# The turned rows in two steps with early masked values, and another weight and hold for the last two pairs' chains

## The chip, the core and the metric

The kernel runs on one core of a Trainium2 chip. A run's time is the device time in microseconds of one execution. The profile shows one execution of the program as recorded by the hardware profiler: TensorE (PE for matmuls, PEld for its weight loads), VectorE (DVE), ScalarE (ACT), GpSimd (POOL) and SyncE (SP, here the issuer of DMAs).

## The reference

The kernel computes a two-layer streaming encoder on 512 frames of 1024 features in float32. Layer A mixes time with a gated recurrence (12 heads of 64) beside a four-head attention into 256 memory tokens; layer B uses chunked attention beside another memory attention. After each mixer comes an output projection and a gated feed-forward block with a three-tap convolution. The change touches only layer A's recurrence:

```python
def wkv7_scan(r, w, k, v, a, b):
    ...
    def step(state, inp):
        r_t, w_t, k_t, v_t, a_t, b_t = inp
        sa = jnp.einsum('bhvk,bhk->bhv', state, a_t)
        state = (state * w_t[:, :, None, :] + sa[..., None] * b_t[:, :, None, :]
                 + v_t[..., None] * k_t[:, :, None, :])
        return state, jnp.einsum('bhvk,bhk->bhv', state, r_t)
    s0 = jnp.zeros((bsz, nh, hd, hd), jnp.float32)
    _, ys = lax.scan(step, s0, xs)
```

Here `a` is the negative normalised key and `b` that key times a learned gate. The result is normalised per head, a bonus term is added, and the whole is multiplied by a gate.

## The kernel before

The 512 frames form eight chunks of 64, and the 12 heads form six pairs (0 to 5), two heads to the 128 partitions. Inside a chunk the recurrence becomes small matmuls; only a short chain runs from chunk to chunk. Three generators do a pair's work.

`prepare(i)` projects the pair's r, k, v and gates: lora-gate matmuls (L740 to L743), then dense matmuls in three products (L204, L205 with the high half of the weights, L208 with the low half). It scans the decay on VectorE (L778) and exponentiates it on ScalarE (L779, L781, with a copy L780). It then makes the key scores (L807); ScalarE copies them (L812), SyncE writes them to DRAM (L815) and reads them back turned as `Lr` (L821); VectorE solves small triangular systems in a chain of short instructions (L830 to L843); the result goes through DRAM again (L849) and returns as `Tc` (L853).

`front(i)` makes the masked chunk scores `ML` (matmuls L898, eviction on VectorE L901), then the turned rows: `rows_av()` turns a and v for the even chunks in two banks (`ev`, L923/L925, copies L928) and the odd chunks in one (`od`, L932/L935, copies L938); `rows_kb()` turns the keys (L913, copies L916). After that it waits for the next pair's scores and extends the inverse to 32 rows (L968, L985, with the copies L974, L977 and L990 of `Y` and `Tt` on ScalarE).

`back(i)` extends the inverse to 64 rows and applies it: transposes on VectorE (L1017); b1X (L1022, copies L1027); the masked values, a product of `ML` and `VT` (L1031, copies L1033); b2Tt (L1038, copies L1042); b3W (L1046, copies L1048 and L1050); b4MQ (L1056, evicted on VectorE by L1058 and L1060); b5G (L1067, L1068, and the copy L1069); b6y (L1077). The chunk-to-chunk chain follows (L1082 on TensorE, L1083 on VectorE, L1087 for the output), then the head norm (L1091 to L1098, sums L690, and via L696 the transposes L699), the bonus and the gate (L1105 to L1116).

All short matmuls write to banks of one PSUM pool with four banks, handed out in turn in program order. Two more pools hold dense results and the chain.

The order is set by `weave()`. It holds a list of generators with a weight each. A generator that is not on hold and has used the smallest share of its weight goes next; each `yield cost` or `yield cost, hold` adds cost to a common clock, and hold keeps the generator back for that much of it. In this way the program order of all instructions is fixed when the kernel is built, and each engine executes its own in a fixed order. In the stages 0 to 4 of the first mixer, `weave` joins the front of pair s, the preparation of pair s + 1, and the back of pair s - 1:

```python
gens = [(front(st_, Ts[st_], Ts[st_ + 1]), 1.069 * FRONT_COST), (prepare(st_ + 1, Ts[st_ + 1]), .971 * PREP_COST)]
if st_ > 0:
    gens.insert(0, (back(st_ - 1, Ts[st_ - 1], dst_mix), 1.003 * BACK_COST))
weave(gens, tc)
```

In this text a stage runs from one L740 to the next; stage 2 begins at 116.0 us, stage 3 at 169.0. The last weave (L1215 to L1223) joins the back of pair 4, the chain of front and back of pair 5, the memory queries and attention, and the first part of the output projection. The dense matmuls of the others are what TensorE has between the short steps.

Of the kernel before, what the change touches and what calls it, by code (L numbers as in the profile page):

```python
# [18 lines left out]
P = 128  # L19
# [63 lines left out]
def weave(gens, tc=None):  # L83

    live = [[g[0], float(g[1]), 0.0, 0.0, g[2] if len(g) > 2 else 0, None] for g in gens]
    now = 0.0
    while live:
        free = [e for e in live if e[5] is None or e[5]()]  # L90
        ready = [e for e in free if e[3] <= now]
        if not ready:
            now = min(e[3] for e in free)
            continue
        e = min(ready, key=lambda x: x[2] / x[1])
        e[5] = None
        try:
            with tc.high_priority(e[4]) if e[4] else ExitStack():
                y = next(e[0])
        except StopIteration:  # L100
            live.remove(e)
            continue
        if callable(y):
            e[5] = y
            continue
        cost, wait = y if isinstance(y, tuple) else (y, 0)
        now += cost
        e[2] += cost
        e[3] = now + wait
# [3 lines left out]
def trunk_kernel(ctx, tc, A, out):  # L113
    nc = tc.nc
    PE, V, SC, GP = nc.tensor, nc.vector, nc.scalar, nc.gpsimd
# [29 lines left out]
    def ps_s(shape=(P, S)):  # L145
        return banks["S"].tile(list(shape), F32, name="pss", tag="pss")
# [355 lines left out]
    HS = (top, bot)  # L502
# [47 lines left out]
    for m in range(KD):  # L550
        nc.sync.dma_start(xs[m // 2][:, m % 2], A["xT"][:, m])
        if m in (0, 2):
            u = slice(m * 256, m * 256 + 512)
# [150 lines left out]
    MC = 16 * 80  # L704
# [7 lines left out]
    def four():  # L712

        for c2 in range(4):
            for par in range(2):
                for h in range(2):
                    c = c2 * 2 + par
                    yield c, c2, par, h, slot(c, h)

    def par_of(t, par):  # L720

        return t.rearrange("p (a e) t -> p a e t", e=2)[:, :, par]
# [164 lines left out]
    def front(i, T, nxt=None):  # L887
        v, KB, AR, Tt, Lc, Tc = c3(T["v"][:]), T["KB"], T["AR"], T["Tt"], T["Lc"], T["Tc"]

        ML = kt_("ML", (P, 2, NCH, 192), bufs=2)  # L890

        for c4 in range(2):
            ps = [ps_s((P, 4, 128)) for _ in range(2)]
            for c in range(4):
                cc = c4 * 4 + c
                for h in range(2):
                    u = slot(cc, h)
                    PE.matmul(ps[h][:, c], KB[HS[h], cc, 1 - u:3 - u].rearrange("p s t -> p (s t)"),  # L898
                              AR[HS[h], cc].rearrange("p s t -> p (s t)"), start=True, stop=True)
            for h in range(2):  # L900
                V.tensor_tensor(ML[:, h, c4 * 4:c4 * 4 + 4, 0:128], ps[h][:],  # L901
                                C("m1").unsqueeze(1).to_broadcast([P, 4, 128]), op=ALU.mult)
            yield 1000
        Rq = kt_("Rq", (P, 8, 64), bufs=2)
        SC.copy(Rq[:], AR[:, :, 1, :])
        VT = kt_("VT", (P, 3, NCH, 64), bufs=2)

        def rows_kb():
            ps = [ups(), ups()]
            for c in range(8):  # L910
                for h in range(2):
                    u = slot(c, h)
                    PE.transpose(ps[h][:, c], KB[HS[h], c, 1 - u:3 - u].rearrange("p s t -> p (s t)"),  # L913
                                 cst[HS[h], I64:I64 + 64])
            for h in range(2):
                SC.copy(ML[:, h, :, 128:192], ps[h][:])  # L916


        def rows_av():
            ev = [ps_s((P, 4, 128)) for _ in range(2)]  # L920
            for c2 in range(4):
                for h in range(2):
                    PE.matmul(ev[h][HS[h], c2, 0:64], AR[HS[h], c2 * 2, 0], cst[HS[h], I64:I64 + 64], start=True, stop=True)  # L923
                for h in range(2):
                    PE.matmul(ev[h][HS[1 - h], c2, 0:64], v[HS[h], c2 * 2], C("blkc", h * 64, 64)[HS[h]],  # L925
                              start=True, stop=True)
            for h in range(2):
                SC.copy(par_of(VT[:, h], 0), ev[h][:, :, 0:64])  # L928
            od = ps_s((P, 2, 4, 64))
            for c2 in range(4):  # L930
                for h in range(2):
                    PE.matmul(od[HS[h], h, c2], AR[HS[h], c2 * 2 + 1, 0], cst[HS[h], I64:I64 + 64],  # L932
                              start=True, stop=True)
                for h in range(2):
                    PE.matmul(od[HS[h], 1 - h, c2], v[HS[h], c2 * 2 + 1], C("blkc", h * 64, 64)[HS[h]],  # L935
                              start=True, stop=True)
            for n in range(2):
                SC.copy(par_of(VT[:, n], 1), od[:, n])  # L938

        rows_av()  # L940
        yield 1000
        rows_kb()
        yield 800


        if nxt is not None:
            yield lambda: "scores" in nxt
        else:
            yield 0, 9000

        def tied():
            order = ExitStack()
            for ins in (dense_at[0],) if nxt is None else (nxt["keys"], *nxt["scores"]):
                order.enter_context(tc.issue_after(ins.ins))
            return order

        Tn = kt_("Tn", (P, NCH, 32))
        with tied():
            tn = V.transpose(Tn[:].rearrange("p c s -> p (c s)"), Tc[:].rearrange("p c s -> p (c s)"))
        if nxt is None:  # L960
            tc.keep_in_program_order(tn)
        ps = ps_s((P, 8, 16))
        for c2 in range(0, 8, 2):
            with tied():
                for c in (c2, c2 + 1):
                    for u in range(4):
                        rw = slice(u * 32, u * 32 + 32)
                        PE.matmul(ps[rw, c], Lc[rw, c], Tc[rw, c, 16:32], start=True, stop=True,  # L968
                                  tile_position=(u * 32, u * 32))
            if c2 < 6:  # L970
                yield 200
        Y = kt_("Y", (P, NCH, 16))
        with tied():
            SC.copy(Y[:], ps[:])  # L974
            for u in range(4):
                rw = slice(u * 32, u * 32 + 32)
                tt = SC.copy(Tt[rw, :, u % 2 * 32:u % 2 * 32 + 32], Tc[rw])  # L977
                if nxt is None and u == 0:
                    tc.keep_in_program_order(tt)
        yield 200, 600  # L980
        ps = ps_s((P, 8, 16))
        for c in range(8):
            for u in range(4):
                rw = slice(u * 32, u * 32 + 16)
                PE.matmul(ps[rw, c], Tn[rw, c, 0:16], Y[rw, c], start=True, stop=True, tile_position=(u * 32, u * 32))  # L985
            if c in (1, 3, 5):
                yield 200
        for u in range(4):
            rw = slice(u * 32, u * 32 + 16)
            SC.copy(Tt[rw, :, u % 2 * 32 + 16:u % 2 * 32 + 32], ps[rw])  # L990
        yield 200
        T.update(Rq=Rq, ML=ML, VT=VT)

    FRONT_COST = 2 * 1000 + 1000 + 3 * 800

    def own_tiles():

# [12 lines left out]
    def back(i, T, dst, tiles=own_tiles, go=None):  # L1010
# [3 lines left out]
        for par in range(2):  # L1014
            for h in range(2):
                u = h ^ par
# [7 lines left out]
        for par in range(2):  # L1024
            for h in range(2):
                hi_ = slice(h * 64 + 32, h * 64 + 64)
                SC.copy(par_of(X5[hi_], par), ps[par][hi_, :, 0:32])  # L1027
        yield 650
        ps = [ps_s((P, 4, 128)) for _ in range(2)]
        for c, c2, par, h, u in four():  # L1030
            PE.matmul(ps[par][HS[h], c2, 0:64], ML[HS[1 - u], h, c, 0:64], VT[HS[1 - u], u, c], start=True, stop=True)  # L1031
        for par in range(2):
            SC.copy(par_of(VT[:, 2], par), ps[par][:, :, 0:64])  # L1033
        yield MC / 2
        ps = ups()
        for c, h, ap, vp in U:
            lo, hi_ = slice(h * 64, h * 64 + 32), slice(h * 64 + 32, h * 64 + 64)
# [12 lines left out]
                SC.copy(par_of(VT[HS[u], u], par), ps[par][HS[u], :, 1])  # L1050
        yield 1100
        G, St = VT[:, 2], W
        yield 0, 900
        ps = [ps_s((P, 4, 128)) for _ in range(2)]
        for c, c2, par, h, u in four():
            PE.matmul(ps[par][HS[h], c2], W[HS[u], c], ML[HS[u], h, c, 64:192], start=True, stop=True)  # L1056
# [8 lines left out]
        for c, h, ap, vp in U:  # L1065
            u = slot(c, h)
# [41 lines left out]
        dst(i, yc, pg)  # L1108
        yield 1080

    BACK_COST = 2 * 650 + 1.5 * MC + 2 * 1100 + 1700 + 6 * 150 + 7 * 150 + 700 + 1080

    mixd = dp.tile([4, P, S], F32, name="mixd", tag="mixd")

# [26 lines left out]
    def chain(*gs_):  # L1141
        for g in gs_:
            yield from g
# [59 lines left out]
    over = set()  # L1203

    def later(ns):
        yield 0, ns

    def told(g, n):
        yield from g
        over.add(n)  # L1210

    def ahead():
# [2 lines left out]

    AHEAD = [0, 1, 2, 3, 4, 6, 7]
    a_, b_ = NPAIR - 2, NPAIR - 1
    weave([(told(back(a_, Ts[a_], dst_mix), "back"), 1.5 * BACK_COST),
           (chain(front(b_, Ts[b_]), later(6000), back(b_, Ts[b_], dst_mix, other_tiles, lambda: "back" in over)),
            1.5 * (FRONT_COST + BACK_COST)),  # L1220
           (told(chain(q_mem(lambda f: A["wA"][18 + f], hact, qmA), flush_mix(), mA), "mem"),
            16 * 648 + mem_cost(860)),
           (ahead(), 14 * 648)], tc)  # L1223
# [346 lines left out]
```

## Time and profile before

| | before |
|---|---|
| median of three runs | 1351.67 us (1349.16, 1351.67, 1352.93) |
| the profiled execution's own time | 1350.19 us |
| its span in the trace | 1348.4 us |
| mean granted TensorE clock | 0.989 |
| DMA | 135.41 MB, mean 100 GB/s |

In the views that follow, a row of a timeline gives the start in us, the duration in us, the engine, the line, the operation, the tile written and those read, and in brackets the idle time of that engine before the row and what ended it. Rows of consecutive equal instructions are joined (x8). A row by window gives its length, then the busy time of PE, PEld, DVE, ACT and POOL, the granted clock (1.00 is full), the DMA share and GB/s.

### The profile page before, as it was taken

How to read it: one execution, taken by the hardware profiler on the slowest of the kernel's cores; microseconds unless marked ns; L12 is line 12 of the kernel's file. 1: busy time of each engine (PE TensorE's matmuls, PEld its weight loads, DVE VectorE, ACT ScalarE, POOL GpSimd, SP SyncE). 2: the span in 40 equal slices, each digit the busy share in tenths (PEclk: the TensorE clock that was granted, in tenths of full speed). 3: DMA queues.
4: the chain of work that ended last, by engine and by line, in shares of the span. 5: the costliest groups of instructions: out<-in, count | busy, mean ns of one | idle time of the engine just before them, and what ended most of it. 6: DMA issues, size and time to landing. Idle time of an engine off the chain costs nothing. (4 is left out here: it accounts for less than half of the span.)

```text
span 1348.4 us, 24498 instructions
## 1 busy us (share of the span) xinstructions
PE 1311.2 (97%) x9838; PEld 1099.4 (82%) x9838; DVE 927.0 (69%) x1834; ACT 688.8 (51%) x1196; POOL 20.5 (2%) x45
## 2 busy tenths in 40 slices
PE   9998999999999999999999999999999999999996
PEld 6786777777788899998888878787788999988886
DVE  7966566765568998889333666658589888893224
ACT  6666556756445444456222566657444444562221
POOL 0000000000000000000000000000000000000000
PEclk9999999999999999999999999999999999999998
DMA  5365333433042432322323422232224222223322
GB/s 195 109 185 106 76 86 85 112 85 88 1 172 83 136 123 66 124 65 88 102 86 91 157 87 80 86 109 86 94 78 156 93 96 95 94 75 100 102 86 77
DMA packets 65729, 135.41 MB, mean 100 GB/s; under 512 B 19792, under 2 KB 25296, under 8 KB 65616
## 3 DMA queue, kind: packets, MB, share of 16 engines
q1 hardware_dynamic: 63168, 124.94, 29.4%
q0 software_dynamic: 2448, 8.91, 3.7%
q8 instruction: 77, 1.26, 0.4%
q14 instruction: 36, 0.29, 0.1%
HBM read 127.53 MB, written 6.29 MB: 99 GB/s over the span
## 5 line engine op out<-in xcount | busy, mean ns | idle before, releaser
L176 DVE TENSOR_TENSOR wlo<-wraw,whi 128x1024 fp32r<-128x1024 f32 (+1 forms) x139 | 165.6, 1192 | 143.9 <-PE psd L208 131.6
L170 ACT CAST whi<-wraw 128x1024 fp32r<-128x1024 f32 (+1 forms) x156 | 159.8, 1026 | 162.0 <-DMA wraw<-in_ffn_out_dram 42.0
L204 PE MATMUL psd<-r1h,whi 128*128 128x512 f32 (+1 forms) x383 | 152.9, 401 | 0.1
L205 PE MATMUL psd<-r1l,whi 128*128 128x512 f32 x320 | 126.7, 397 | 0.0
L170 ACT CAST whi<-raw 128x1024 fp32r<-128x1024 f32 x88 | 82.9, 943 | 80.7 <-PE psf L420 45.5
L176 DVE TENSOR_TENSOR wlo<-raw,whi 128x1024 fp32r<-128x1024 f32 x88 | 95.8, 1088 | 15.5 <-ACT whi L170 15.2
L208 PE MATMUL psd<-r1h,wlo 128*128 128x512 f32 (+1 forms) x383 | 103.3, 396 | 0.0
L204 PEld LDWEIGHTS psd<-r1h,whi 128*128 128x128 f32 x383 | 72.3, 189 | 16.2 <-issue 1.7
L208 PEld LDWEIGHTS psd<-r1h,wlo 128*128 128x128 f32 x383 | 68.6, 188 | 13.4 <-issue 0.2
L420 PE MATMUL psf<-r2l,whi 128*128 128x256 f32 x308 | 77.2, 283 | 0.0
L420 PE MATMUL psf<-r2h,whi 128*128 128x256 f32 x308 | 77.2, 283 | 0.0
L204 PE MATMUL psd<-r2h,whi 128*128 128x512 f32 (+1 forms) x184 | 71.1, 390 | 0.1
L238 ACT ACTIVATE tmp<-xT 128x512 f32<-128x512 f32 x27 | 17.1, 632 | 104.8 <-DVE xT L497 89.0
L205 PEld LDWEIGHTS psd<-r1l,whi 128*128 128x128 f32 x320 | 60.5, 189 | 11.6 <-issue 0.5
L205 PE MATMUL psd<-r2l,whi 128*128 128x512 f32 (+1 forms) x184 | 69.9, 383 | 0.0
L420 PEld LDWEIGHTS psf<-r2l,whi 128*128 128x128 f32 x308 | 59.1, 192 | 0.2
L420 PEld LDWEIGHTS psf<-r2h,whi 128*128 128x128 f32 x308 | 59.1, 192 | 0.2
L422 PE MATMUL psf<-r2h,wlo 128*128 128x256 f32 x308 | 49.5, 283 | 0.0
L208 PE MATMUL psd<-r2h,wlo 128*128 128x512 f32 (+1 forms) x184 | 47.1, 386 | 0.0
L204 PE MATMUL psd<-hl,whi 128*128 128x512 f32 (+1 forms) x119 | 44.4, 377 | 0.0
L205 PE MATMUL psd<-sl,whi 128*128 128x512 f32 (+1 forms) x119 | 44.4, 377 | 0.0
L205 PE MATMUL psd<-hl,whi 128*128 128x512 f32 (+1 forms) x119 | 44.3, 376 | 0.0
(473 smaller groups left out, 3323.4 us busy)
## 6 DMA issues: line engine op xcount, KB each, us to landing
wraw<-in_ffn_in_dram SPq DMA_DIRECT2D x44, 512.0 KB, 3.7
raw<-in_ffn_in_dram SPq DMA_DIRECT2D x88, 256.0 KB, 3.8
wraw<-in_ffn_out_dram SPq DMA_DIRECT2D x32, 448.0 KB, 3.3
wraw<-in_wA_dram SPq DMA_DIRECT2D x20, 512.0 KB, 4.3
wraw<-in_w_out_dram SPq DMA_DIRECT2D x16, 512.0 KB, 3.9
wraw<-in_ffn_out_dram SPq DMA_DIRECT2D x16, 512.0 KB, 3.5
wlo<-in_wA_dram POOLq DMA_DIRECT2D x15, 512.0 KB, 7.7
wraw<-in_wB_dram SPq DMA_DIRECT2D x8, 512.0 KB, 3.5
```

The lines of the kernel that those rows point to most:

```text
L170: SC.copy(hi[:, :n], raw)
L176: V.tensor_tensor(lo[:, :n], raw, hi[:, :n], op=ALU.subtract)
L204: PE.matmul(ps, wh[:, j * P:(j + 1) * P], ah, start=start and n == 0, stop=False)
L205: dense_at[0] = PE.matmul(ps, wh[:, j * P:(j + 1) * P], al, start=False, stop=False)
L208: dense_at[0] = PE.matmul(ps, wl[:, j * P:(j + 1) * P], act(k)[0], start=False, stop=stop and n == len(ks) - 1)
L238: SC.activation(sq[:], src, AF.Square)
L420: PE.matmul(ps, wh[:, o + k * P:o + k * P + P], x[k][n], start=k == n == 0, stop=False)
L422: PE.matmul(ps, wl[:, o + k * P:o + k * P + P], x[k][0], start=False, stop=k == 3)
```

## The change

Four things change; no instruction is added, removed or given another shape.

- The turned rows become two steps: `rows_av()` now ends after the even chunks, and the odd chunks are a function of their own, `rows_odd()`, with a yield between, and `rows_kb()` comes last. There are holds of 1000 after the first step and after the keys.
- The masked values move from `back()` to `front()`, behind the turned keys. In `back()` the yield after b1X becomes `400, 800`.
- In `back()` the hold before b4MQ goes from 900 to 2000.
- In the last weave both chains get 4 in place of 1.5 as the factor of their weight, and the hold between the last pair's front and back goes from 6000 to 2000. The cost totals follow the moved yields.

```diff
         rows_av()
-        yield 1000
+        yield 550, 1000
+        rows_odd()
+        yield 1080
         rows_kb()
-        yield 800
+        yield 800, 1000
+        ps = [ps_s((P, 4, 128)) for _ in range(2)]
+        for c, c2, par, h, u in four():
+            PE.matmul(ps[par][HS[h], c2, 0:64], ML[HS[1 - u], h, c, 0:64], VT[HS[1 - u], u, c], start=True, stop=True)
+        for par in range(2):
+            SC.copy(par_of(VT[:, 2], par), ps[par][:, :, 0:64])
+        yield MC / 2
...
-    FRONT_COST = 2 * 1000 + 1000 + 3 * 800
+    FRONT_COST = 2 * 1000 + 1630 + 3 * 800 + MC / 2
...
                 SC.copy(par_of(X5[hi_], par), ps[par][hi_, :, 0:32])
-        yield 650
-        ps = [ps_s((P, 4, 128)) for _ in range(2)]
-        for c, c2, par, h, u in four():
-            PE.matmul(ps[par][HS[h], c2, 0:64], ML[HS[1 - u], h, c, 0:64], VT[HS[1 - u], u, c], start=True, stop=True)
-        for par in range(2):
-            SC.copy(par_of(VT[:, 2], par), ps[par][:, :, 0:64])
-        yield MC / 2
+        yield 400, 800
...
-        yield 0, 900
+        yield 0, 2000
...
-    BACK_COST = 2 * 650 + 1.5 * MC + 2 * 1100 + 1700 + 6 * 150 + 7 * 150 + 700 + 1080
+    BACK_COST = 400 + 650 + MC + 2 * 1100 + 1700 + 6 * 150 + 7 * 150 + 700 + 1080
...
-    weave([(told(back(a_, Ts[a_], dst_mix), "back"), 1.5 * BACK_COST),
-           (chain(front(b_, Ts[b_]), later(6000), back(b_, Ts[b_], dst_mix, other_tiles, lambda: "back" in over)),
-            1.5 * (FRONT_COST + BACK_COST)),
+    weave([(told(back(a_, Ts[a_], dst_mix), "back"), 4 * BACK_COST),
+           (chain(front(b_, Ts[b_]), later(2000), back(b_, Ts[b_], dst_mix, other_tiles, lambda: "back" in over)),
+            4 * (FRONT_COST + BACK_COST)),
```

In the changed file the lines behind the turned rows move by up to ten: `od` is L934/L937, the masked values L950 with the copies L952, b1X L1032, b2Tt L1042, b3W L1050, b4MQ L1060, b5G L1071, b6y L1081, the chain L1086. In the prediction a line's number is that of the kernel before, unless it says otherwise.

More of the change, by code (lines that the diff above doesn't have):

```diff
@@ L928, in rows_av, with rows_odd @@
                 SC.copy(par_of(VT[:, h], 0), ev[h][:, :, 0:64])
+        def rows_odd():
             od = ps_s((P, 2, 4, 64))
```

## The prediction

> **What bounds the kernel now.** I read the page first, then the waits of TensorE, then the busy time by window, cut at the first lora-gate matmul (L740) of each stage, and last the timelines of the few places where TensorE idles. A difference under 0.3% (4 us) cannot be told from no change here.
>
> ```profile
> PE 1311.2 (97%) x9838; PEld 1099.4 (82%) x9838; DVE 927.0 (69%) x1834; ACT 688.8 (51%) x1196; POOL 20.5 (2%) x45
> ```
> ```profile
> PE pss L932 <- DVE MQ L1060: 5.0, 4, 3.9
> PE pss L1056 <- ACT W L1048: 2.8, 6, 0.7
> ```
> ```profile
> 116.00:169.00 53.00, 46.57 (x668) 35.65 (x666) 31.63 (x106) 30.04 (x61) 3.45 (x4) 0.94 0.41 88
> 169.00:213.60 44.60, 42.11 (x655) 31.91 (x654) 29.77 (x97) 28.38 (x60) 2.59 (x3) 1.00 0.41 93
> ```
>
> The two waits listed are TensorE's longest around the change (total us, times, longest). TensorE is busy 97% of the span, so the kernel is as long as its matmuls, TensorE's idle time, and what a low granted clock adds. The change keeps every instruction and its shape; only the order moves. So I count just idle time and clock in the stages of the first mixer. In the windows (columns: length, busy PE, PEld, DVE, ACT, POOL, granted clock, DMA share, GB/s) stage 2 (116 to 169) takes 53.0 us and stage 3, with the same kinds of work, 44.6; the granted clock is 0.94 against 1.00. That 8.4 us is the one large loss that an order could give back.
>
> **Stage 2: what the loss is, and what the change does to it.**
>
> ```profile
> 113.10 0.35 SPq L181 DMA_DIRECT2D wraw<-in_wA_dram  x1
> 113.62 1.73 SPq L821 DMA_DIRECT2D Lr<-d  x4
> ```
> ```profile
> DMA to landing us min/median/max: 1.6/1.8/6.9
> ```
> ```profile
> 121.83 0.36 DVE L830 TENSOR_TENSOR Xu<-Lr,cst 128x120 f32<-128x120 f32 x1 [2.17 <-DMA Lr<-d]
> ```
> ```profile
> 121.34 1.48 PE L1046 MATMUL pss<-VT,Tt 64*64 64x128 f32 x32 [1.35 <-ACT Tt L1042]
> 132.05 0.48 PE L932 MATMUL pss<-cst,AR 64*64 64x64 f32 x4 [3.86 <-DVE MQ L1060]
> ```
> ```profile
> 58.00:60.00 2.00, 0.00 (x0) 0.00 (x0) 2.00 (x5) 1.29 (x2) 0.00 (x0) 1.00 0.34 43
> 62.00:64.00 2.00, 1.74 (x9) 1.74 (x10) 2.00 (x5) 1.90 (x6) 0.00 (x0) 0.64 0.08 8
> 64.00:66.00 2.00, 2.00 (x11) 2.00 (x11) 2.00 (x3) 0.17 (x1) 0.00 (x0) 0.51 0.17 17
> 132.00:134.00 2.00, 1.95 (x33) 1.86 (x33) 0.56 (x2) 1.28 (x3) 0.00 (x0) 0.50 0.66 94
> ```
>
> SyncE issues a weight load of 512 KB and then the four small reads of Lr (L821). One of these took 6.9 us to land where the median is 1.8. VectorE therefore starts its chain on Lr (L830 to L843) only at 121.83; the evictions of MQ stand behind that chain on VectorE, and L932, which takes MQ's banks, waits 3.86 us for them. After that gap the clock stood at 0.50. With the 1.35 us of L1046 the stage loses 5.2 us of idle, and the rest, 3.2 of the 8.4, is the half clock.
>
> In the changed kernel as built, SyncE lists the four Lr reads ahead of that weight load, and ScalarE lists the copies of the lora scores that feed them ahead of an L762 that stood before them. With the median landing instead of 6.9, Lr arrives about 5 us earlier, the chain on VectorE ends before MQ is wanted, and the Tt copy (L1042, now L1046) no longer stands behind the exponentials L779 and L781. I take 6.5 us of the 8.4: all of it less the 1.9 that the new wait at a stage's head, priced below, costs in this stage too. The bounds are 8.4, and nothing if the late landing comes from something other than that load. Moving the load behind the reads costs SyncE's queue 1.73 us; weights are buffered ahead, so I take nothing, at most that 1.7.
>
> **Heads of stages 3, 4 and 5: a wait is added.** The listed order after the norm transposes (L699) was: L1031, b2Tt (L1038), scores (L898), b3W (L1046), three dense, b4MQ (L1056), ev (L923/925), od (L932/935). It becomes: b2Tt, three L208 and a dense, b3W, scores, ev, b4MQ, one dense, b5G (L1067), two dense, od.
>
> ```profile
> 163.77 1.98 PE L208 MATMUL psd<-r1h,wlo 128*128 128x512 f32 x8
> 166.28 0.63 PE L699 MATMUL pss<-cst,tmp 128*128 128x128 f32 x4 [0.53 <-DVE tmp L696]
> 170.11 0.68 PE L1031 MATMUL pss<-VT,ML 64*64 64x64 f32 x16
> 171.77 0.69 PE L1038 MATMUL pss<-Tt,X 32*32 32x32 f32 x32
> 173.49 1.10 PE L1046 MATMUL pss<-VT,Tt 64*64 64x128 f32 x32
> 174.52 0.50 PE L205 MATMUL psd<-r1l,whi 128*128 128x512 f32 x1
> 176.21 0.65 PE L1056 MATMUL pss<-ML,W 64*64 64x128 f32 x6 [0.72 <-ACT W L1048]
> 177.25 0.77 PE L1056 MATMUL pss<-ML,W 64*64 64x128 f32 x19 [0.39 <-ACT W L1048]
> 179.11 0.33 PE L932 MATMUL pss<-cst,AR 64*64 64x64 f32 x4 [0.31 <-DVE MQ L1060]
> ```
> ```profile
> 164.90 0.69 DVE L882 TENSOR_TENSOR bon<-pss,v 128x512 f32<-128x512 f32 x1
> 172.63 1.23 DVE L778 TENSOR_TENSOR_SCAN tmp<-acc,tmp 128x512 f32<-128x512 f32 x1
> ```
> ```profile
> 175.79 0.37 ACT L1048 COPY W<-pss 128x256 f32<-128x256 f32 x1
> 177.09 0.74 ACT L1050 COPY VT<-pss 64x256 f32<-64x256 f32 x2
> ```
>
> There are four small banks, taken in turn, so ev takes the two banks of b3W, which the copies L1048/L1050 free. Those copies stand on ScalarE behind three instructions that wait for the decay scan (L778); they ended at 177.83, 11.55 us after L699 began. Without the L1031 block TensorE reaches ev sooner: before, L699 to the end of b3W took 8.24 us (166.28 to 174.52); less the L1031 block and the dense matmul inside it (170.11 to 171.77, 1.66) and plus five L208 (0.25 each from the row of eight), one dense and the bonus matmuls (2.1 together, the last 0.85 an estimate) it is about 8.65. The scan is no earlier, and with L882 moved behind L696 about 0.6 later (0.69 by its row), so the copies end at about 12.2. ev alternates between its two banks and must wait for the last one: 3.3 us idle, and about 0.5 more at b4MQ, whose banks are freed by an eviction (L901) that is listed near the end of VectorE's chain. Before, the same stretch idled 0.72 + 0.39 + 0.31 = 1.4. The net is 2.4 per stage; if the scan is not later it is 1.4. I take 1.9, so 5.7 for three stages (bounds 0 and 7.2: at zero, the copies are as early as TensorE).
>
> The gap may also drop the clock: an idle of about 2.2 us around 58 to 60 was followed by 0.64 and 0.51 at 62 to 66, and the 3.86 above by 0.50. Stage 2's half clock cost 3.2, so I price one fall at 2 us and give it an even chance: 3 us over three stages (0 to 6). [...]
>
> **The tail (pairs 4 and 5, 295 to 366).** Weights of 4 and a hold of 2000 put the chains in front of the dense work.
>
> ```profile
> 309.51 0.39 PE L205 MATMUL psd<-r1l,whi 128*128 128x512 f32 x1
> 309.74 0.39 PE L204 MATMUL psd<-r1h,whi 128*128 128x512 f32 x1
> 295.59 0.66 PE L699 MATMUL pss<-cst,tmp 128*128 128x128 f32 x4 [0.35 <-DVE tmp L696]
> 300.18 1.16 PE L898 MATMUL pss<-AR,KB 64*128 64x128 f32 x16 [0.50 <-DVE ML L901]
> 323.48 0.33 PE L1082 MATMUL psl<-W,MQ 64*64 64x64 f32 x4 [0.55 <-DVE W L1083]
> 334.15 1.98 PE L1046 MATMUL pss<-VT,Tt 64*64 64x128 f32 x32
> ```
> ```profile
> 295.45 0.74 DVE L763 SCALAR_TENSOR_TENSOR v<-tmp,vec,v 128x511 f32<-128x511 f32 x1
> 296.11 0.34 DVE L830 TENSOR_TENSOR Xu<-Lr,cst 128x120 f32<-128x120 f32 x1
> 297.77 0.79 DVE L836 SCALAR_TENSOR_TENSOR Xsb<-Lr,Xsb 128x14 f32<-128x14 f32 x5
> 328.40 1.28 DVE L1017 STREAM_TRANSPOSE AR<-Tt 32x128 f32<-32x128 f32 x4
> ```
> ```profile
> 312.11 1.39 ACT L977 COPY Tt<-Tc 32x256 f32<-32x256 f32 x3 [0.72 <-DMA Tc<-d2b]
> ```
> ```profile
> 332.00:342.00 10.00, 10.00 (x125) 7.62 (x119) 3.83 (x11) 4.99 (x17) 0.00 (x0) 0.51 0.17 54
> ```
>
> Before, dense matmuls (0.23 us each, 309.51 to 309.74) lie between nearly all steps, and waits on this stretch add up to about 2.4 us. After, L696 stands on VectorE behind L760, four transposes, L763, L830 to L836 and two more, by the rows above 0.74 + 0.34 + 0.79 + 1.28 and, estimated from their like, 1.4 for the rest: 4.5 us. Sixteen dense and three L208 (16 x 0.23 + 3 x 0.25 = 4.4) stand on TensorE for that and for the rsqrt steps ahead of it, which at 0.2 us each of some eight (estimated) take 1.5: 1.6 idle. Then come, with no dense work between, the second scores and ev waiting for L901 (2.1 by the 0.5 of 300.18 for each of four steps), b4MQ and b5G (0.7), and the first state step, whose W copy stands on ScalarE behind L977's wait for a DMA (1.6): 6.0. The last pair's b-steps, listed without memory scores between them, add about 3. So 9.0 - 2.4 = +6.6 (bounds: 2, if VectorE catches up, and 11). The clock can go either way: at 332 to 342 it stood at 0.51 after state steps and memory scores with only the short waits shown, and L1046 took 1.98 instead of 1.10, so about 4.5 us was lost there; the dip may go, or a second one may come at 301 to 316 (+3). I net these to -0.6, so the tail is +6.
>
> **Sum.** -6.5 + 5.7 + 3 + 6 = +8.2 on the profiled 1350.19, which is 1358.4 us; that execution lies 1.5 under the median of 1351.67 and inside the three runs. Predicted: 1358.5.
>
> **Rivals.** *The dips decide, faster.* Stage 2 gives 6.5, the 332 dip goes (-4.5) since memory work now interleaves with the state steps, the copies are hardly late (+1.5 in three stages), and the tail idles half of my sum (+3.3): -6.2, so 1344. For it: both dips are in the trace, and every idle I add rests on listed order alone. Against: ev needs both banks. It decides if W's copies come before about 9.2 us after L699. Chance 0.24. *It cancels.* Stage 2 gives 6.5, the heads cost 5.7 with no clock fall because no gap reaches 3.86 us, the one gap of this length in stage 2, and the tail's 6.6 loses the dip of 4.5: +1.3, so 1351.5. Chance 0.20. [...] *The clock falls everywhere:* three heads and the tail, +3 and +3 more: 1365. Chance 0.14. *The change does not do what it says in stage 2:* Lr still lands late, and since L830 now stands ahead of the scan, the scan waits too: the 6.5 is lost and the heads cost the same, 1365. Chance 0.05.
>
> **How the numbers follow.** My forecast has 0.37; with the last two, slower has 0.56, same 0.20, faster 0.24. The range reaches from the faster case to a little past the clock case: 1343.5 to 1367.5. The forecast's own range is 1354 to 1363.
>
> **What would show it.** Right: stage 2 near 46 us with no half clock, L821 landing near 1.8 us at most; ev (L923) waiting on W or VT copies by 2 to 3.5 us in stages 3, 4 and 5; L699 waiting 1 to 2 us near 296; L977's successor late. Wrong: stages 3 to 5 at or below 44.6 us, or no dip after 330.

## Result: slower by 0.3%, half of what was summed

| | before | after |
|---|---|---|
| median | 1349.17 us (20 runs, 1347.66 to 1352.93) | 1353.31 us (20 runs, 1347.68 to 1359.08) |
| ratio | | 1.0032, 95% interval 1.0021 to 1.0044 |
| profiled execution | 1350.19 us, span 1348.4 | 1352.74 us, span 1351.0 |

The 20 runs of the changed kernel spread over 11 us, those before over 5, and by and large the longer runs have the lower granted clock: 0.994 in the one of 1347.68 us, 0.983 in the one of 1359.08. The clock goes with the spread: the correlation of span with (1 - clock) x span over the 20 runs is 0.93.

The busy times and TensorE's longest waits around the change, after:

```profile
PE 1313.0 (97%) x9838; PEld 1101.3 (82%) x9838; DVE 925.6 (69%) x1834; ACT 688.9 (51%) x1196; POOL 20.2 (1%) x45
```
```profile
PE pss L923 <- ACT VT L1054: 5.0, 6, 1.1
PE psl L1086 <- ACT W L1073: 3.8, 1, 3.8
PE pss L699 <- DVE tmp L696: 1.9, 5, 0.7
PE pss L995 <- issue: 1.5, 2, 1.0
```

The waits on MQ (5.0) and on W (2.8) that were shown before are gone, and ev (L923) waits in their place, six times, 5.0 us in all. One single wait of 3.8 us is new. Stages 2, 3 and 4, cut again at L740:

```profile
117.75:163.71 45.96, 45.01 (x668) 33.82 (x667) 32.81 (x108) 29.21 (x60) 2.59 (x3) 1.00 0.47 100
163.71:208.46 44.75, 42.25 (x655) 32.01 (x654) 29.96 (x97) 28.15 (x59) 2.59 (x3) 1.00 0.40 92
208.46:255.41 46.95, 43.52 (x655) 33.18 (x654) 29.98 (x97) 28.37 (x59) 2.59 (x3) 0.96 0.39 84
```

The differences between the two profiles, from one L740 to the next: start +1.5 (ahead of every line that the change touches; a piece of half clock that costs 1.7 us stands there at 9), stages 0 and 1 +0.2 together, stage 2 -7.0 (52.95 to 45.96), stage 3 +0.15, stage 4 +2.35, and from stage 5's L740 to the end of the span +5.4 (1090.21 to 1095.59). Together +2.6, which is the difference of the spans. The medians differ by 4.1, because the profiled run before lies 1.0 above its median and the one after 0.6 below.

The stretch behind stage 5's L740 can be parted at the next norm transposes (L699, at 295.59 before and 296.62 after), where the tail of the prediction begins:

```profile
258.19:295.59 37.40, 35.47 (x586) 27.03 (x585) 26.01 (x82) 24.33 (x52) 1.72 (x2) 1.00 0.34 81
255.41:296.62 41.21, 37.77 (x598) 28.91 (x597) 26.60 (x91) 25.89 (x53) 2.59 (x3) 1.00 0.40 89
```

The first row is before, the second after. More matmuls stand in this part after the change, so its length tells nothing. TensorE's idle time does: 3.4 us in place of 1.9. So 1.5 of the 5.4 belongs to stage 5 with its head, and 3.9 to what lies behind it, the tail.

The reads of Lr for stage 2 on SyncE's queue, and the time that all such reads took to land, after:

```profile
113.62 1.70 SPq L821 DMA_DIRECT2D Lr<-d  x4
115.48 0.35 SPq L181 DMA_DIRECT2D wraw<-in_wA_dram  x1
```
```profile
DMA to landing us min/median/max: 1.6/2.9/4.2
```

The reads stand ahead of the weight load now, as forecast. The head of stage 3, after, on TensorE and on ScalarE:

```profile
159.24 0.66 PE L699 MATMUL pss<-cst,tmp 128*128 128x128 f32 x4 [0.32 <-DVE tmp L696]
160.67 0.50 PE L208 MATMUL psd<-r1h,wlo 128*128 128x512 f32 x1
161.10 1.15 PE L898 MATMUL pss<-AR,KB 64*128 64x128 f32 x8
...
166.57 1.47 PE L1050 MATMUL pss<-VT,Tt 64*64 64x128 f32 x32
167.97 1.16 PE L898 MATMUL pss<-AR,KB 64*128 64x128 f32 x16
170.10 0.27 PE L923 MATMUL pss<-cst,AR 64*64 64x64 f32 x1 [0.97 <-ACT VT L1054]
171.13 0.27 PE L923 MATMUL pss<-cst,AR 64*64 64x64 f32 x1 [0.59 <-ACT VT L1054]
```
```profile
170.34 0.74 ACT L1054 COPY VT<-pss 64x256 f32<-64x256 f32 x2
```

ev waits for the last copies of b3W, as forecast, but for 1.56 us and not 3.3. In stages 4 and 5 it waits 1.65 and 1.76:

```profile
214.85 0.27 PE L923 MATMUL pss<-cst,AR 64*64 64x64 f32 x1 [1.06 <-ACT VT L1054]
215.89 0.27 PE L923 MATMUL pss<-cst,AR 64*64 64x64 f32 x1 [0.59 <-ACT VT L1054]
261.64 0.33 PE L923 MATMUL pss<-cst,AR 64*64 64x64 f32 x2 [1.05 <-ACT VT L1054]
262.67 0.27 PE L923 MATMUL pss<-cst,AR 64*64 64x64 f32 x1 [0.71 <-ACT VT L1054]
```

And in the tail, the new large wait, on ScalarE and on TensorE, and then the granted clock:

```profile
313.02 1.40 ACT L987 COPY Tt<-Tc 32x256 f32<-32x256 f32 x3 [3.72 <-DMA Tc<-d2b]
314.44 0.24 ACT L1073 COPY W<-VT 128x64 f32<-128x64 f32 x1
```
```profile
314.74 0.33 PE L1086 MATMUL psl<-W,MQ 64*64 64x64 f32 x4 [3.78 <-ACT W L1073]
```
```profile
216.00:218.00 2.00, 2.00 (x56) 1.70 (x56) 1.80 (x7) 1.83 (x4) 0.00 (x0) 0.80 1.00 194
218.00:220.00 2.00, 2.00 (x25) 1.46 (x25) 1.24 (x4) 0.75 (x2) 0.00 (x0) 0.50 0.69 113
316.00:318.00 2.00, 2.00 (x12) 1.26 (x8) 0.87 (x2) 0.58 (x1) 0.00 (x0) 0.55 0.01 4
334.00:336.00 2.00, 2.00 (x30) 1.67 (x29) 1.96 (x7) 0.69 (x3) 0.00 (x0) 0.50 0.59 217
```

ScalarE takes L1073 behind three copies that wait 3.72 us for a DMA; TensorE has no other work ahead of it in its order. Half clock follows that gap at 316, comes once in stage 4 (217 to 221) and again at 333 to 341.

### The profile page after: what moved, and what is told of

It reads as the page before. It is cut to its first block, busy times and chain, and to the rows that moved or that the text cites. A ratio compares the mean times of both kernels' runs of the same rounds, so it can differ in the third digit from the quotient of the medians.

```text
span 1351.0 us, 24483 instructions
## 1 busy us (share of the span) xinstructions
PE 1313.0 (97%) x9838; PEld 1101.3 (82%) x9838; DVE 925.6 (69%) x1834; ACT 688.9 (51%) x1196; POOL 20.2 (1%) x45
## 5 line engine op out<-in xcount | busy, mean ns | idle before, releaser
L208 PE MATMUL psd<-r1h,wlo 128*128 128x512 f32 (+1 forms) x383 | 106.5, 400 | 0.0
L208 PEld LDWEIGHTS psd<-r1h,wlo 128*128 128x128 f32 x383 | 68.8, 189 | 13.9 <-issue 0.2
L422 PE MATMUL psf<-r2h,wlo 128*128 128x256 f32 x308 | 49.5, 283 | 0.0
L208 PE MATMUL psd<-r2h,wlo 128*128 128x512 f32 (+1 forms) x184 | 47.1, 386 | 0.0
L204 PE MATMUL psd<-hl,whi 128*128 128x512 f32 (+1 forms) x119 | 44.4, 377 | 0.0
L420 PE MATMUL psf<-r1h,whi 128*128 128x256 f32 x176 | 44.2, 284 | 0.2 <-ACT tmp L442 0.2
```

The source lines that it names most:

```text
L204: PE.matmul(ps, wh[:, j * P:(j + 1) * P], ah, start=start and n == 0, stop=False)
L208: dense_at[0] = PE.matmul(ps, wl[:, j * P:(j + 1) * P], act(k)[0], start=False, stop=stop and n == len(ks) - 1)
L420: PE.matmul(ps, wh[:, o + k * P:o + k * P + P], x[k][n], start=k == n == 0, stop=False)
L422: PE.matmul(ps, wl[:, o + k * P:o + k * P + P], x[k][0], start=False, stop=k == 3)
```

## The measure that the experiments use

Summed over windows of 1 us, 1 - clock is taken here as the time that a stretch of half clock takes away; before, the 32 matmuls of b3W took 1.10 us at a clock of 1.00 (at 173.49) and 1.98 at 0.50 (at 334.15). Ahead of the kernel's last microseconds it comes in pieces of 1.7 us, or two, three or six times that, in the profiles of both kernels and of e9 to e14: 3.4 us at half clock lose 1.7. Before, it was 1.7 at 62, 3.4 at 130 to 138, 5.1 at 332 to 343; after, 1.7 at 9, 63, 217 and 316, 3.4 at 333.

So each run can be parted into (1 - clock) x span and the rest. A run's clock is on record to 0.001, which is 1.35 us, so differences of about 1 us in the last two columns mean nothing. Medians in us, over the runs of each kernel:

| kernel | span | lost to the clock | rest |
|---|---|---|---|
| before | 1348.3 | 14.8 | 1333.2 |
| changed | 1351.5 | 16.9 | 1335.1 |
| e1 changed, old weave | 1357.2 | 23.1 | 1334.8 |
| e2 before, new weave | 1351.4 | 13.5 | 1338.6 |
| e3 changed, state copy on VectorE | 1348.1 | 15.5 | 1332.9 |
| e4 before, Lr reads first | 1354.7 | 21.0 | 1334.1 |
| e5 two-step rows alone | 1342.9 | 20.1 | 1323.1 |
| e6 early masked values alone | 1350.4 | 17.6 | 1333.1 |
| e7 both moves, hold 900, old weave | 1356.1 | 20.3 | 1335.1 |
| e8 e1 with one filler | 1362.1 | 23.8 | 1338.2 |
| e9 two-step rows, new weave | 1343.8 | 15.5 | 1328.7 |
| e10 e9, hold 0, state copy | 1337.5 | 10.0 | 1328.0 |
| e11 e9, factors 2.5, state copy | 1333.5 | 9.3 | 1324.2 |
| e12 e11 with hold 0 | 1342.3 | 14.8 | 1327.2 |
| e13 e1 with four fillers | 1357.6 | 12.9 | 1344.9 |
| e14 changed, rows in one step | 1348.5 | 15.5 | 1333.2 |

## Experiments

**e1 and e2: the last weave by itself.**

```diff
-    weave([(told(back(a_, ... ), 4 * BACK_COST), (chain(front(b_, ...), later(2000), ...), 4 * (FRONT_COST + BACK_COST)),
+    weave([(told(back(a_, ... ), 1.5 * BACK_COST), (chain(front(b_, ...), later(6000), ...), 1.5 * (FRONT_COST + BACK_COST)),
```

That is e1, on the changed kernel; e2 is the same lines the other way round, on the kernel before.

> The changed kernel with the last weave as it was (factors 1.5, hold 6000). Theory A (the parts add up: stage 2 gives 7 us, the last weave takes them back with interest): the tail's 5.4 us go, so 1347 to 1349 us against the changed kernel's 1353.3, and the wait of 3.8 us at the first state step is gone. Rival B (the new wait at the heads of stages 3 to 5 and the clock falls behind it carry the loss, the tail does not): 1352 to 1354, and single runs spread by about 10 us as they do now.

> The kernel before with only the last weave changed (factors 4, hold 2000). Theory A: 1349.2 plus about 5, 1353 to 1356 us; stages 2 to 4 as before (53.0, 44.6, 44.6). Rival B: 1348 to 1350.

Measured: e1 1358.89 us, 1.0068 (1.0054 to 1.0083) of the kernel before; e2 1353.14 us, 1.0022 (1.0008 to 1.0037). Theory A foresaw e2 and failed on e1, which is slower than the changed kernel by 5.6 us in the medians (4.9 by the two ratios to the kernel before); B's figures fit neither. The parts do not add up. On the kernel before (e2), the new weave costs 5.4 us of rest and saves 1.3 of clock; on the new front and back it costs 0.3 of rest and saves 6.2 of clock. Two windows of e1 show where its clock goes:

```profile
320.00:350.00 30.00, 28.41 (x257) 18.25 (x256) 16.98 (x53) 13.94 (x47) 0.00 (x0) 0.54 0.07 21
350.00:356.00 6.00, 5.25 (x108) 4.22 (x106) 4.96 (x12) 4.68 (x15) 0.00 (x0) 1.00 0.00 0
```

TensorE is busy for 28.4 of 30 us and has a clock of 0.54. Between its small steps stand memory scores (L1203) and transposes (L303); the first dense rows, three of 128x512, come at 338. But TensorE had also idled for 2.7 us in three waits between 315.7 and 322.1, and the clock fell at 321, so e1 alone cannot tell idle time from small matmuls. e8 below can.

Stage 2 of e2 has the program order of the kernel before and took 50.06 us, not 52.95, with one piece of half clock (1.7 us) in place of two. So a stage of one program differs by 2.9 us between two runs.

**e3: the wait of 3.8 us.**

```diff
-        SC.copy(St[:, 1], G[:, 0])
+        (V.tensor_copy if i == NPAIR - 2 else SC.copy)(St[:, 1], G[:, 0])
```

> The changed kernel, but in the back of pair 4 the copy of the first state (L1073) runs on VectorE, where nothing is queued, in place of ScalarE, where it stands behind three copies that wait for a DMA. Theory A: the wait of 3.8 us and the half clock behind it go, 1348 to 1350 us. Rival C (the wait only moves, to the next step that needs that DMA): 1352 to 1354.

Measured: 1349.88 us, 0.9998 (0.9984 to 1.0013). Against the changed kernel that is -3.4 us in the medians (-4.6 by the ratios): rest -2.2, clock -1.4. That is Theory A's time, and the wait is gone and came up nowhere else. The half clock at 316 went too, but a longer one came at 326 to 339 (6.8 us lost in this profile, with TensorE busy throughout), so the second half of Theory A does not hold. One copy queued behind a DMA wait on ScalarE accounts for about as much as the whole change costs.

**e4: stage 2's queue.**

```diff
+            if i == 1: lr_at.append(lr)    # lr: the last of the four L821 reads
...
-        nc.sync.dma_start(raw[:, :n], src)
+        with tc.issue_after(lr_at.pop().ins) if lr_at else ExitStack(): nc.sync.dma_start(raw[:, :n], src)
```

> The kernel before with one order changed: in stage 1 the weight load that stood ahead of the four small reads of Lr on SyncE's queue is issued behind them. Theory A (stage 2's 8.4 us come from that queue): stage 2 takes 45 to 47 us in place of 53.0, no half clock, 1342 to 1344 us. Rival D (stage 2 got shorter by the new order of the matmul steps): stage 2 stays near 53, 1348 to 1350; if the weights come too late now, TensorE waits for them and it is slower than before.

Measured: 1356.45 us, 1.0051 (1.0036 to 1.0066); stage 2 took 54.93. The reads landed in 3.9 us at most, and the price was elsewhere (this file's lines lie one or two further):

```profile
124.14 0.58 PE L205 MATMUL psd<-r1h,whi 128*128 128x512 f32 x1 [1.39 <-ACT whi L170]
132.07 2.11 PE L209 MATMUL psd<-r1h,wlo 128*128 128x512 f32 x8 [1.16 <-DMA wlo<-in_wA_dram]
```

The weights that were put back are late now, so this run cannot show what the early reads are worth by themselves.

**e5, e6 and e7: the moves one by one, with the old last weave.** The edits of e5 and e6 against the kernel before, and of e7 against e1:

```diff
         rows_av()
-        yield 1000
+        yield 550, 1000
+        rows_odd()
+        yield 1080
         rows_kb()
-        yield 800
+        yield 800, 1000
```
```diff
         rows_kb()
         yield 800
+        ps = [ps_s((P, 4, 128)) for _ in range(2)]
...
+        yield MC / 2
```
```diff
-        yield 0, 2000
+        yield 0, 900
```

In e6 the same block leaves `back()`, whose yield after b1X is `400, 800`, as in the change.

> The kernel before with only the turned rows in two steps (masked values, hold and last weave as before). Here the small Lr reads stand ahead of the weight load on SyncE, as in the changed kernel. Theory E (each 1.7 us of clock is one 3.4-us stretch at half clock; the long half-clock stretch at 321 to 349 comes from the last pair's steps and the memory scores standing without dense matmuls between them, which hold and masked values bring about): stage 2 near 46 us, tail near 1090, so 1343 to 1346 us. Rival F (the two-step rows themselves thin out the tail): tail 1098 or more, 1350 to 1357.

> The kernel before with only the masked values moved to the front (rows in one step, hold 900, last weave as before). Theory E: the tail has a longer half-clock stretch than the kernel before (5 us lost there before), 1350 to 1356. Rival F: tail as before, 1343 to 1346 with stage 2 near 46.

> The changed kernel with the last weave as it was and the hold before b4MQ back at 900, so the two moves of the rows and of the masked values together. If the hold of 2000 brings the long half-clock stretch: 1347 to 1351. If the hold does nothing: 1357 to 1360 like the run with the hold of 2000 and the old weave.

Measured: e5 1344.70 us, 0.9962 (0.9949 to 0.9975); e6 1352.16 us, 1.0007 (0.9989 to 1.0024); e7 1357.84 us, 1.0065 (1.0049 to 1.0080). So the two-step rows alone make the kernel faster by 5 us; the early masked values on top take 13 us back; the hold of 2000 does next to nothing (e1 against e7, 1 us). Theory E's times for e5 and e6 came out, but the tail of e5 is rival F's: it is 8.6 us longer than before, with 13.7 us of clock lost at 310 to 338. The gain sits in the stages: 43.68, 42.28 and 41.98 us for stages 2 to 4, where the kernel before has 52.95, 44.60 and 44.60. Stage 2 is short with the masked values alone as well: 45.92 us in e6 (46.61 with both moves, e7). The head of stage 3 in e5:

```profile
165.43 1.10 PE L1050 MATMUL pss<-VT,Tt 64*64 64x128 f32 x32
166.46 1.88 PE L208 MATMUL psd<-r1h,wlo 128*128 128x512 f32 x7
168.27 0.27 PE L923 MATMUL pss<-cst,AR 64*64 64x64 f32 x2
```

Seven dense matmuls stand between b3W and ev, and ev waits for nothing. In the changed kernel the masked values no longer stand at the head, the order uses up those dense matmuls ahead of b3W, and ev waits.

**e8 and e13: what the half clock hangs on.**

```diff
+        for _ in range(4): PE.matmul(ps, gsh[:, 0:128], gsh[:, 0:256], start=True, stop=True)
         PE.matmul(ps, qmA[f][HS[hh], qc], kmT0[HS[hh], f], start=True, stop=True)
```

This is e13, against e1; e8 has one such matmul per score.

> The changed kernel with the old last weave, and ahead of each of the memory scores one useless dense matmul (128x128 by 256 columns) into the same bank, which the score then overwrites: work is added, 16 times about 0.13 to 0.25 us, 2 to 4 us at full clock. Theory E (the clock falls there because the array has little to do in the small matmuls, not because TensorE idles): the 13.6 us lost at 321 to 349 shrink by 5 or more, and the time is the same or lower than 1358.9 in spite of the added work, 1350 to 1358. Rival G (the clock falls on idle gaps alone): the stretch stays at half clock and the added work costs 3 to 6 us, 1361 to 1365.

> As the run with useless dense matmuls ahead of the memory scores, but four (128x128 by 256 columns) for each score in place of one: 64 of about 0.11 to 0.13 us, 7 to 8 us of added work at full clock over the changed kernel with the old last weave. Theory E (what the array is given to do sets the clock): the half-clock stretch at 321 to 349 mostly goes, 1352 to 1362 us. Rival G (only idle gaps set it, or nothing that filler can change): the added work runs at half clock, 1370 us or more.

Measured: e8 1363.90 us, 1.0095 (1.0079 to 1.0112), the stretch still at half clock, as rival G has it. With four, 1359.47 us, 1.0075 (1.0057 to 1.0094), and no half clock in the stretch at all. First the fall in e8:

```profile
310.00:322.00 12.00, 12.00 (x180) 8.83 (x177) 4.52 (x11) 5.69 (x13) 0.81 (x1) 1.00 0.68 189
322.00:324.00 2.00, 2.00 (x69) 1.21 (x69) 2.00 (x5) 0.00 (x0) 0.00 (x0) 0.89 0.00 0
324.00:326.00 2.00, 2.00 (x24) 1.30 (x12) 1.55 (x6) 1.72 (x8) 0.00 (x0) 0.50 0.00 0
```

By the profile TensorE is busy in all of the 13 us ahead of it; the fall comes some 5 us after the last of its dense rows of 128x512 (L208, up to 318.24). The same window, e8 and then e13:

```profile
320.00:350.00 30.00, 29.54 (x283) 18.33 (x285) 14.97 (x44) 12.50 (x43) 0.00 (x0) 0.56 0.06 21
```
```profile
320.00:350.00 30.00, 29.92 (x387) 19.97 (x385) 18.85 (x57) 16.48 (x52) 0.00 (x0) 1.00 0.07 22
```

TensorE is busy to 98% and more in both. 48 more useless matmuls bring the clock from 0.56 to 1.00 and make the kernel 4.4 us faster in the medians (2.7 by the ratios to the kernel before); against e1, 10.1 us of rest are added and 10.2 of clock come back. So idle time alone does not set the clock of this stretch: at nearly the same busy share, 16 added matmuls left it at 0.56 and 64 brought it to 1.00. Two or three per score were not tried.

**e14: the changed kernel with the rows in one step.** The edit takes e5's lines out again:

```diff
-        yield 550, 1000
-        rows_odd()
-        yield 1080
+        yield 1000
         rows_kb()
-        yield 800, 1000
+        yield 800
```

> The changed kernel with the turned rows in one step again: early masked values, hold 2000, new last weave. Theory H (the two-step rows pay in full only where the masked values stay as cover): 1350 to 1358, stages 3 and 4 near 44 to 47, within 3 us of the changed kernel. Rival: the two-step rows carry 5 us here as well, 1358 or more.

Measured: 1350.23 us, 1.0010 (0.9993 to 1.0027), 3.1 us faster than the changed kernel in the medians, with intervals that overlap, and not slower: beside the early masked values the two-step rows are worth nothing. Its profile is that of the slowest of its 12 runs (1359.47 us, clock 0.982). There its Lr reads also stand ahead of the load and VectorE does not wait for them, yet stage 2 takes 49.67 us, with this wait and half clock behind it:

```profile
128.87 1.97 PE L1056 MATMUL pss<-ML,W 64*64 64x128 f32 x28 [2.40 <-ACT VT L928]
```

The half clock in this stage, 128 to 136, costs 3.4 us. Without it stage 2 would be 46.3, close to the changed kernel's 45.96.

**e9 to e12: a better version.** Two-step rows and the new last weave (e9), with the masked values and the hold before b4MQ as in the kernel before; e10, e11 and e12 have e3's line too and vary the factors and the hold.

```diff
-    weave([(told(back(a_, ... ), 1.5 * BACK_COST), (chain(front(b_, ...), later(6000), ...), 1.5 * (FRONT_COST + BACK_COST)),
+    weave([(told(back(a_, ... ), 2.5 * BACK_COST), (chain(front(b_, ...), later(2000), ...), 2.5 * (FRONT_COST + BACK_COST)),
```

(e11; e10 has 4 and hold 0, e12 has 2.5 and hold 0.)

> The changed kernel without the early masked values and with the hold of 900: turned rows in two steps and the new last weave (factors 4, hold 2000). Theory H (the two-step rows give 10 us at full clock, the early masked values take them back by leaving the wait of the even rows without cover, and the new weave breaks up the half-clock stretch of 13.7 us): stages 2 to 4 near 43.7, 42.3, 42.0 as with the rows alone, tail 1091 to 1095, so 1337 to 1342 us. Rival I (the new weave costs as much idle time, 5 us, as it saves in clock, as it did on the kernel before): 1343 to 1347, the same as with the rows alone.

> As the run with the two-step rows and factors 4, but hold 0 before the last pair's back, and the copy of pair 4's first state on VectorE. Theory H: dense matmuls stand between more of the last pair's steps, tail 1088 to 1092, 1335 to 1340 us. Rival I: 1343 to 1347.

> Two-step rows, factors 2.5, hold 2000, the copy of pair 4's first state on VectorE. Theory H: less idle time than with factors 4, some more half clock: 1337 to 1342. Rival I: 1343 to 1347.

> Two-step rows, factors 2.5, hold 0, the copy of pair 4's first state on VectorE. Theory H: 1335 to 1341, the best of these if the state steps with dense matmuls between keep the clock. Rival I: 1343 to 1347.

Measured: e9 1345.52 us, 0.9968 (0.9958 to 0.9978); e10 1339.29, 0.9922 (0.9902 to 0.9943); e11 1335.28, 0.9889 (0.9872 to 0.9906); e12 1344.05, 0.9961 (0.9946 to 0.9975). Rival I holds for e9, theory H for e10 and, with room, for e11; e12 was expected among the best and is not: its time is rival I's. The stages came out as in e5 in all four. e9 and e11, 300 to 350:

```profile
300.00:350.00 50.00, 46.73 (x561) 31.72 (x562) 25.53 (x83) 24.57 (x67) 0.86 (x1) 0.78 0.21 56
```
```profile
300.00:350.00 50.00, 47.43 (x612) 31.71 (x610) 31.22 (x96) 29.12 (x80) 0.86 (x1) 1.00 0.20 56
```

In its profile e11 has no half clock between 66 and 1322 us, and TensorE waits less in its tail; it is faster than both kernels. Which of its lines brings how much was not parted.

## Why the prediction was wrong

The forecast was slower, and slower it is, inside the range; the size was wrong: +8.2 summed against +4.1 in the medians and +2.6 between the profiles. By its steps:

- *Stage 2, -6.5:* -7.0 in the profiles. The reads are early, VectorE does not wait for Lr, and the MQ wait is gone, though the reads landed in 2.9 us in the median and 4.2 at most, not 1.8. The size is luck in part, since stage 2 of the order before took 50.06 in e2. Less its half clock, stage 2 is 49.5 before and 48.4 in e2, and 43.7 to 46.3 in the kernels with the reads ahead in which the rows or the masked values moved (e5, e6, e14, changed). e4 moves the reads alone and has 51.4, but there the weights came 2.6 us late, against the 1.7 at most that the prediction gave to moving the load. So what the early reads bring by themselves stays open.
- *Heads, +5.7 of idle and +3 of clock:* this step failed. Over the three heads +4.0 was measured (stage 3 +0.15, stage 4 +2.35, stage 5 +1.5 of idle) in place of +8.7. The wait of ev is there, and its cause is the one forecast, but it is 1.56, 1.65 and 1.76 us, not 3.3, and it took the place of waits of 1.42, 1.41 and 1.16: together +1.0. In stage 3 TensorE reached ev 9.9 us after L699 (159.24 to 169.13), not 8.65. A single L208 between small matmuls takes 0.43 us from its start to the next (160.67 to 161.10) where a row of eight gives 0.25; b3W after a dense one takes 1.40 (166.57 to 167.97), not 1.03; and the first scores, cut in two by an L208, take 2.18 (161.10 to 162.19 and 162.62 to 163.71), where they took 1.77 in one row. The copies ended at 11.8, not 12.2. The 0.5 at b4MQ is not there. In the profile the clock fell in one of three heads (stage 4, 1.7 us lost); that and 1.0 us of idle at L995, which the profile gives no cause for, cover stage 4's +2.35. The lower value of the net wait was also mis-summed: less the scan's 0.6, 2.4 gives 1.8 and not 1.4. Against the two-step rows alone (e5), the lack of cover at the heads is dear, 2.5 us in stage 3; against the kernel before, which has a wait of that size already, it is not.
- *Tail, +6:* +3.9 in the profile, by other terms. L699 waited 0.66, not 1.6; the scores, ev, b4MQ and b5G waited 0.45 together, not 2.8; the first state step 3.78, not 1.6, and e3 shows 3.4 us for it. The clock lost 5.1 us here in both profiles (332 to 342 before; 316 and 333 after). The sign of the weave's part was wrong: on the new front and back it saves 5.6 us (e1).
- *The clock:* it was priced as the result of gaps. e8 shows that a stretch of small matmuls loses it without a gap (0.50 after 13 us with no idle time), and e13 that 64 dense matmuls among them keep it (1.00 over 30 us); the prediction's own row at 332 to 342 had pointed there. With that, a sum over waits alone could not find this kernel's time.

The rival in which gains and stalls cancel came nearest, 1351.5 against 1353.31. That is luck in part: stage 2's gain came as it says, but its heads were 5.7 and came to 4.0, and its dip of 4.5 at 332 became two dips that cost the same together. Nor did its reason for no clock fall at the heads hold: in stage 4 the clock fell at 217, behind waits of 1.06 and 0.59 us and none of 3.86.

## What to carry to other kernels

Change orders one part at a time: here one part was worth 5 us, another cost 13 beside it, and a third paid only because of the second. When a step is moved off a place where an engine waits, ask which independent work will stand there instead; and look for copies queued behind a DMA wait on the same engine (here 3.78 us of TensorE's time). Where small matmuls follow each other in a long row, here for some 30 us at a clock of 0.54 with TensorE 95% busy (e1), read the granted clock beside the busy share, and try dense matmuls among them (1.00 in e13).

## What the runs showed of the hardware

- TensorE, 95% busy among small matmuls, had a mean clock of 0.54 over 30 us (e1). With 16 dense matmuls added it fell to 0.50 after 13 us without any idle time (e8); with 64 it stayed at 1.00 (e13).
- Ahead of the last microseconds the half clock came in pieces of 3.4 us, 1.7 us lost each, from one piece to six in a row (both kernels, e9 to e14). Over the 20 runs of the changed kernel (1 - clock) x span went from 8.1 to 23.1 us, and the spread of 11 us goes with it (correlation 0.93).
- In four kernels with the new last weave TensorE was idle for 0.8 us (changed kernel), 1.3 (e14), 1.8 (e3) and 2.3 us (e2) near 323 to 328 us, with no cause in the profile. e10, e11 and e12 show 0.3 to 1.9 us near 310, and e9 none. This stays open.
